# The even layer's output projection as seven half-size products with early operand sums

## The chip, the cores and the metric

The kernel runs on one core of a Trainium2 chip. The metric is device time in microseconds for one launch. A core has a matrix engine (TensorE, PE in the profile), VectorE (DVE), ScalarE (ACT), GpSimd (POOL), SyncE (SP), which issues the DMAs here, and 16 DMA engines. Matmuls read on-chip memory (SBUF) and add into PSUM banks of 128 x 512 floats.

## The reference

A decoder trunk of two layers on x of 1024 rows (s) and 1024 columns (d), in float32:

```
even: h = x @ e_w_in; A = Griffin RG-LRU of h; B = stick-breaking attention of 8 heads
      y = concat(A * silu(gate), B * silu(gate))                  # 1024 x 2048
      x1 = LayerNorm(alpha * x + y @ e_w_out)                     # e_w_out: 2048 x 1024
odd:  sliding-window attention of 16 heads with sinks, gate, output projection,
      out = LayerNorm(alpha * x1 + ...)
```

The change concerns `y @ e_w_out` with the sum and the LayerNorm (LN) around it.

## The kernel before

Every float32 product is made of three matmuls: each operand is split into a high part h (a cast) and a low part l (operand minus h), and h·h, h·l and l·h are added in one PSUM bank (`mm3`, L109). A split costs one cast and one subtraction, for weights on GpSimd (`load_piece`, L102 and L103).

The stages follow each other: loads, the recurrence half A with its projections (to about 315 us), eight attention heads (n = 0 to 7), the even output projection, the odd layer's projections with the sliding-window stage, and the odd output projection. An attention head is cut into 12 units. For a unit, TensorE makes z (L289 to 291), ScalarE two exponentials B and C, GpSimd sets one column of C (MEMSET, L299), VectorE makes the running sum C (L305) and the product B (L307), TensorE transposes B (tr, L315), and pv multiplies it by the values (L332 to 338). Between these TensorE works on filler: in heads 0 to 6 the input projections of the next head, in head 7 `early_out`.

y is kept in DRAM, split: `split_y_half` (L255) casts on ScalarE (L258), subtracts on VectorE (L259) and stores both parts. Tiles of y are named yhla and yhlb when they are made, yla and ylb when they are loaded again. The output projection (`out_proj`, L535; banks named ope) runs over 16 pieces of the contraction of 2048. For each of the two column halves (dm) and each block of 128 rows (s, eight of them) a bank is filled by 16 pieces of three matmuls 128 x 512. `early_out` (L482) does ten pieces for three row blocks of the first column half while head 7 is still running. When attention has ended, the LN constants (gb, L645), the rest of y (L267) and x (xpre, L658) are loaded, and weights (wr_e, L93) follow piece by piece. After each block of rows VectorE adds the bank to alpha * x (L544), LN runs over VectorE, ScalarE and GpSimd (`ln_a`, `ln_b`, `ln_c`), and TensorE transposes the result for the odd layer (x1tr, L673), which begins with the projections pj_ok, pj_ov and pj_oq.

Engines run their own instructions in order. Their order comes from the order of the program, from a scheduler at compile time, and from pools of tiles that make a writer wait for the last reader: 24 slots of 128 x 2 x 512, three raw tiles for weights, and PSUM banks (three pj, two z, two tr, one pv). All large DMAs are issued by SP into one queue, in order; a DMA waits for the one eight places ahead of it.

Of the kernel before, what the change touches and what calls it, by code (L numbers as in the profile page):

```python
# [18 lines left out]
P = 128  # L19
# [33 lines left out]
def trunk(ctx, tc, x, xT_in, w_even, w_even_v, w_even_out, w_gate, lru_vec,  # L53
# [381 lines left out]
    def lru_main(f):  # L435
# [25 lines left out]
        for hf in range(2):  # L461
# [11 lines left out]
    def yh_even(e, s):
        hl = yhl[("b", e - 8, s // 4) if e >= 8 else ("a", e, s // 4)]
        c = (s % 4) * P
        return hl[:, 0, c:c + P], hl[:, 1, c:c + P]

    EARLY = [13, 0, 1, 2, 3, 4, 5, 6, 7, 14]
    LATE = [8, 9, 10, 11, 12, 15]
    op0 = {}  # L480

    def early_out():  # L482
        for s in range(3):
            op0[s] = bank("pj", f"ope0_{s}")
        for idx, e in enumerate(EARLY):
            wh, wl = load_piece(w_even_out[0, e], f"f0_{e}")
            for s in range(3):
                yh_, yl_ = yh_even(e, s)
# [42 lines left out]
    ACC = ["pj", "pj", "pj", "z", "z", "tr", "tr", "pv"]  # L531
# [3 lines left out]
    def out_proj(w_src, es, yh, n_tail, tail_piece, lnp, gb, after, name, final, early=None):  # L535
# [55 lines left out]

        for dm in range(2):
# [3 lines left out]
            if dm == 0 and early:  # L596
                ps = dict(early[0])
                for ei, group in enumerate(early[1:]):
                    for idx, e in enumerate(group):
                        wh, wl = load_piece(w_src[dm, e], f"{name}{dm}_{e}")  # L600
                        for s in range(NS):
                            if ei == 0 and s in early[0]:
                                continue
                            if s not in ps:
                                ps[s] = bank(ACC[s], f"op{name}{dm}_{s}")
                            yh_, yl_ = yh(e, s)
# [352 lines left out]
```

## Time and profile before

| | us |
|---|---|
| median of three runs (lowest to highest) | 1277.57 (1277.12 to 1277.88) |
| profiled execution | 1275.71 |
| its span, first to last instruction | 1273.7 |
| TensorE busy | 1246.3, 6272 matmuls |
| VectorE, ScalarE, GpSimd busy | 770.1, 577.9, 542.4 |

Busy times are sums over all stages. Since TensorE is busy in 98% of the span, the stages in which it is not, and those in which its granted clock is lower, are to be looked for in the tables by stretches and in the waits. The mean granted clock is 0.996 of the full one.

### The profile page before, as it was taken

How to read it: one execution, taken by the hardware profiler on the slowest of the kernel's cores; microseconds unless marked ns; L12 is line 12 of the kernel's file. 1: busy time of each engine (PE TensorE's matmuls, PEld its weight loads, DVE VectorE, ACT ScalarE, POOL GpSimd, SP SyncE). 2: the span in 40 equal slices, each digit the busy share in tenths (PEclk: the TensorE clock that was granted, in tenths of full speed). 3: DMA queues.
4: the chain of work that ended last, by engine and by line, in shares of the span. 5: the costliest groups of instructions: out<-in, count | busy, mean ns of one | idle time of the engine just before them, and what ended most of it. 6: DMA issues, size and time to landing. Idle time of an engine off the chain costs nothing.

```text
span 1273.7 us, 18009 instructions
## 1 busy us (share of the span) xinstructions
PE 1246.3 (98%) x6272; PEld 1052.6 (83%) x6272; DVE 770.1 (60%) x1661; ACT 577.9 (45%) x1212; POOL 542.4 (43%) x692
## 2 busy tenths in 40 slices
PE   8999999999999999999999979999999999999997
PEld 7888788888888888888888868888788888887886
DVE  7355746645565756766658502036477777878467
ACT  5254555656343433434434300014277777778300
POOL 3333544445323323232234653536455555555440
PEclk9999999999999999999999989999999999999999
DMA  7322332234212222123128571201111111111022
GB/s 253 129 68 84 135 112 87 87 110 147 83 50 84 67 66 92 53 80 98 27 67 336 176 260 52 70 24 34 44 43 32 33 35 34 33 29 64 17 84 99
DMA packets 63306, 110.79 MB, mean 87 GB/s; under 512 B 7280, under 2 KB 25072, under 8 KB 62960
## 3 DMA queue, kind: packets, MB, share of 16 engines
q1 hardware_dynamic: 63216, 109.65, 26.5%
q8 instruction: 50, 0.82, 0.3%
q14 instruction: 40, 0.33, 0.1%
HBM read 83.40 MB, written 26.21 MB: 86 GB/s over the span
## 4 chain that ended last, share of the span: by engine, by line
PE 83%; DVE 6%; ACT 5%; DMA 2%; issue 2%; POOL 1%; SPq 0%; POOLq 0%; ACTq 0%; DVEq 0%
PE ope L110 4%; PE ope L112 4%; PE ope L111 4%; PE tr L315 2%; PE pj_g L110 2%; PE pj_g L111 2%; PE pj_g L112 2%; PE pjv L110 2%; PE pjv L111 2%; PE pjv L112 2%; PE opo L111 2%; PE opo L110 2%; PE opo L112 2%; PE pj_k L112 2%; PE pj_k L111 2%; PE pj_q L110 2%
## 5 line engine op out<-in xcount | busy, mean ns | idle before, releaser
L803 POOL TENSOR_SCALAR S<-S,sm 128x256 f32<-128x256 f32 (+1 forms) x128 | 59.9, 482 | 77.8 <-DVE sm L801 31.9
L553 ACT ACTIVATE rs<-mv,eps_t 128x1 f32<-128x1 f32 x16 | 4.7, 295 | 193.4 <-DVE mv L552 193.4
L296 ACT ACTIVATE C<-z 128x512 f32<-128x512 f32 (+3 forms) x96 | 47.3, 493 | 92.5 <-DVE z L293 77.5
L798 ACT ACTIVATE S<-S,sm 128x256 f32<-128x256 f32 (+1 forms) x128 | 62.6, 490 | 57.5 <-DVE sm L794 53.7
L544 DVE SCALAR_TENSOR_TENSOR xpre<-xpre,ope 128x512 f32<-128x512 f32 x16 | 10.8, 681 | 119.2 <-PE ope L112 119.2
L307 DVE TENSOR_TENSOR B<-B,C 128x512 f32<-128x512 f32 (+3 forms) x96 | 58.4, 608 | 10.5
L344 POOL TENSOR_TENSOR yb<-pvt,yb 128x128 f32<-128x128 f32 x32 | 15.4, 480 | 108.6 <-DVE pvt L343 85.4
L305 DVE TENSOR_TENSOR_SCAN C<-C,one 128x512 f32<-128x512 f32 (+1 forms) x64 | 54.0, 843 | 11.8 <-ACT C L296 11.6
L118 ACT CAST wt<-tr 128x512 fp32r<-128x512 f32 (+3 forms) x96 | 46.7, 486 | 29.5 <-PE tr L315 28.7
L119 DVE TENSOR_TENSOR wt<-tr,wt 128x512 fp32r<-128x512 f32 (+3 forms) x96 | 52.6, 549 | 8.0 <-ACT wt L118 7.6
L110 PE MATMUL pjv<-wv,xh 128*128 128x512 f32 x128 | 49.6, 399 | 6.2 <-ACT wv L219 6.2
L110 PE MATMUL pj_g<-xh,wh_g 128*128 128x512 f32 x128 | 51.9, 406 | 0.4 <-DVE kl L119 0.4
L110 PE MATMUL pj_k<-xh,wh_k 128*128 128x512 f32 x128 | 52.2, 408 | 0.0
L791 DVE CUSTOM_DVE_ANT_0 S<-s,bias 128x256 f32<-128x256 f32 (+1 forms) x128 | 47.4, 403 | 7.7 <-PE s L786 6.9
L110 PE MATMUL pj_og<-x1h,wh_og 128*128 128x512 f32 x128 | 51.9, 406 | 0.0
L110 PE MATMUL pj_q<-xh,wh_q 128*128 128x512 f32 x128 | 51.9, 405 | 0.0
L110 PE MATMUL pj_oq<-x1h,wh_oq 128*128 128x512 f32 x128 | 51.8, 405 | 0.0
L112 PE MATMUL pj_k<-xh,wl_k 128*128 128x512 f32 x128 | 51.6, 403 | 0.0
L111 PE MATMUL pj_og<-x1l,wh_og 128*128 128x512 f32 x128 | 51.0, 398 | 0.0
L111 PE MATMUL pjv<-wv,xh 128*128 128x512 f32 x128 | 50.5, 394 | 0.5 <-DVE wv L220 0.5
L112 PE MATMUL pj_og<-x1h,wl_og 128*128 128x512 f32 x128 | 50.8, 397 | 0.0
L111 PE MATMUL pj_k<-xl,wh_k 128*128 128x512 f32 x128 | 50.6, 395 | 0.0
(317 smaller groups left out, 4334.6 us busy)
## 6 DMA issues: line engine op xcount, KB each, us to landing
vst<-vhl SPq DMA_DIRECT2D x16, 512.0 KB, 3.7
ysta<-yhla SPq DMA_DIRECT2D x16, 512.0 KB, 3.5
yla<-ysta SPq DMA_DIRECT2D x16, 512.0 KB, 10.0
wr_e<-in_w_even_out_dram SPq DMA_DIRECT2D x32, 256.0 KB, 2.7
ystb<-yhlb SPq DMA_DIRECT2D x10, 512.0 KB, 2.9
ylb<-ystb SPq DMA_DIRECT2D x10, 512.0 KB, 6.6
xraw<-in_xT_dram SPq DMA_DIRECT2D x16, 256.0 KB, 5.4
wvraw<-in_w_even_v_dram SPq DMA_DIRECT2D x16, 256.0 KB, 4.3
```

The source lines that it names most:

```text
L110: nc.tensor.matmul(ps, wh, xh, start=start, stop=False)
L111: nc.tensor.matmul(ps, wh, xl, start=False, stop=False)
L112: nc.tensor.matmul(ps, wl, xh, start=False, stop=stop)
L118: nc.scalar.copy(h, ps)
L119: nc.vector.tensor_tensor(out=l, in0=ps, in1=h.bitcast(F32), op=ALU.subtract)
L296: nc.scalar.activation(C[:, :W], z[:, :W], AF.Sigmoid, scale=-SC)
L305: nc.vector.tensor_tensor_scan(cr, cr, one.broadcast_to([P, W]), init, ALU.mult, ALU.mult)
L307: nc.vector.tensor_tensor(out=B[:, :W], in0=B[:, :W], in1=C[:, 1:W + 1], op=ALU.mult)
L315: nc.tensor.transpose(tr[:, t * P:(t + 1) * P], B[:, t * P:(t + 1) * P], ident)
L791: nc.vector.tensor_tensor_reduce(out=Sb[:, j, lo:], in0=ps[:, j, lo:], in1=bias[:, j, lo:], scale=1.0, scalar=-BIG, op0=ALU.add, op1=ALU.m ...
L798: nc.scalar.activation(Sb[:, j, lo:], Sb[:, j, lo:], AF.Exp, bias=nm[:, j:j + 1], accum_out=den[:, j:j + 1])
L803: nc.gpsimd.tensor_scalar(out=Sb[:, j, lo:], in0=Sb[:, j, lo:], scalar1=rec[:, j:j + 1], scalar2=0.0, op0=ALU.mult, op1=ALU.add)
```

## The change

The product of y (1024 x 2048) and the weights (2048 x 1024) is cut in two in each of its three dimensions and made by the Strassen-Winograd scheme: seven products of half size in each dimension instead of eight, on sums and differences of the quarters. A11 and A21 are the two row halves of the recurrence half of y, A12 and A22 those of the attention half; b11, b21, b12 and b22 are quarters of the weights. The sums are

```
S1 = A21 + A22   S2 = S1 - A11 (as A22 - S3)   S3 = A11 - A21   S4 = A12 - S2
T1 = b12 - b11   T2 = b22 - T1 (as T3 + b11)   T3 = b22 - b12   T4 = b21 - T2
```

with the signs that the code gives them. They are made as soon as their parts are there: S3 in the recurrence stage on VectorE, T1 to T4 in each head on GpSimd (`w_sums`: four loads, four operations, four stores), S1, S2 and S4 at the end of each head on GpSimd (`y_sums`). All are kept in DRAM unsplit (`stash`, 256 KB each). `split_y_half` is gone.

The projection is 7 products of 8 steps; a step is 4 blocks of 3 matmuls 128 x 512. `prep(k)` loads the two operands of step k, casts both on ScalarE, and subtracts the y operand on VectorE (opwh) and the weight operand on GpSimd (opwl); it is called nine steps ahead. The products accumulate in two sets of banks: X (three pj and pv; named opeX) and Z (two z and two tr; opeZ), and `evac` adds banks to xpre on the way. `early_out` now does three of the four blocks of the first product. In the last product block by block is finished, with LN and transposes between. The odd layer starts with the second half of the rows. x is loaded in 16 pieces of 256 KB instead of 8 of 512 KB.

```diff
-    def split_y_half(key, hf, raw, keep):
-        hl = slot(f"yhl{key[0]}{key[1]}{hf}", F32R) if key[0] == "b" else \
-            yt(("vh", "vl")[hf], [P, 2, HALF], f"yhla{key[1]}{hf}")
-        nc.scalar.copy(hl[:, 0, :], raw)
-        nc.vector.tensor_tensor(out=hl[:, 1, :], in0=raw, in1=hl[:, 0, :].bitcast(F32), op=ALU.subtract)
...
+    def stash(kind, t, tile_):
+        yst[kind, t] = tc.dram_tile([P, HALF], F32, name=f"st{kind}{t}")
+        nc.sync.dma_start(yst[kind, t], tile_)
+
+    def w_sums(t):
...
+        for tile_, dm, e in ((b22, 1, 8 + t), (b12, 1, t), (b11, 0, t), (b21, 0, 8 + t)):
+            nc.sync.dma_start(tile_, w_even_out[dm, e])
+        sub = partial(nc.gpsimd.tensor_tensor, op=ALU.subtract)
+        sub(out=b22, in0=b22, in1=b12)
+        stash("T3", t, b22)
+        sub(out=b12, in0=b12, in1=b11)
+        stash("T1", t, b12)
+        nc.gpsimd.tensor_tensor(out=b11, in0=b22, in1=b11, op=ALU.add)
+        stash("T2", t, b11)
+        sub(out=b21, in0=b21, in1=b11)
+        stash("T4", t, b21)
...
+    def y_sums(n, hf):
+        y = ytile["b", n][:, hf, :]
+        a21, s3 = ya_in[n][:, 0, :], ya_in[n][:, 1, :]
+        if hf == 1:
+            stash("A22", n, y)
+            nc.gpsimd.tensor_tensor(out=a21, in0=a21, in1=y, op=ALU.add)
+            stash("S1", n, a21)
+            nc.gpsimd.tensor_tensor(out=s3, in0=y, in1=s3, op=ALU.subtract)
+            stash("S2", n, s3)
         else:
+            stash("A12", n, y)
+            s4 = slot(f"s4_{n}", F32)[:, 0, :]
+            nc.gpsimd.tensor_tensor(out=s4, in0=y, in1=s3, op=ALU.subtract)
+            stash("S4", n, s4)
...
+                if (i, g) == (NS - 2, 1):
+                    w_sums(n)
...
-                        for hf in range(2):
-                            for f in range(8):
-                                load_y(("a", f), hf, slot(f"yla{f}{hf}", F32R))
+                        for t in range(8):
+                            prep(t)
                         fill.add(early_out())
-                        rate[0] = 20.4 / 12
+                        rate[0] = 16.4 / 12
...
+    XB, ZB = ["pj", "pj", "pj", "pv"], ["z", "z", "tr", "tr"]
+    PRODUCTS = [("A11", (0, 0), 0), ("S3", "T3", 1), ("S2", "T2", 0), ("A22", "T4", 1), ("S1", "T1", 0),
+                ("A12", (0, 8), 1), ("S4", (1, 8), 0)]
...
+    def prep(k):
...
+            raw = wpool.tile([P, HALF], F32, tag=tag, name=f"raw{tag}{k}", bufs=5)
+            nc.sync.dma_start(raw, src)
+            hl = slot(f"op{tag}{k}", F32R)
+            nc.scalar.copy(hl[:, 0, :], raw)
+            eng = nc.vector if tag == "wh" else nc.gpsimd
+            eng.tensor_tensor(out=hl[:, 1, :], in0=raw, in1=hl[:, 0, :].bitcast(F32), op=ALU.subtract)
...
     def early_out():
...
+        for p in range(3):
+            op[0, p] = bank(XB[p], f"opeX{p}")
+        for t in range(8):
+            for p in range(3):
+                step_mm(t, p)
                 yield C_512
...
+        op[0, 3] = bank(XB[3], "opeX3")
+        for t in range(8):
+            step_mm(t, 3)
+        for k in range(8, 8 + AHEAD):
+            prep(k)
...
+            for p in range(4):
+                for t in range(8):
+                    step_mm(8 * i + t, p)
+                evac(i, p)
+                norm(p)
+                if p in (1, 2):
+                    x1_transposes(p + 1)
```

The next rows are TensorE's at the end of the last head, before: the last attention product (pv_0) with what stands ahead of it and behind it; ope are banks of the projection.

```order
L112 MATMUL ope_5_6979<-wh_e_2_7035,yla_6428 128x512
L110 MATMUL ope_3_6971<-wh_e_3_7056,yla_6414 128x512
L332 MATMUL pv_0_6907<-wt_1_0_6900,vh_5879 128x256
L333 MATMUL pv_0_6907<-wt_1_0_6900,vh_5879 128x256
L334 MATMUL pv_0_6907<-wt_1_0_6900,vl_5880 128x256
L336 MATMUL pv_0_6907<-wt_1_0_6900,vh_5879 128x256
L338 MATMUL pv_0_6907<-wt_1_0_6900,vl_5880 128x128
L110 MATMUL ope_6_6983<-wh_e_13_6967,yhlb_5821 128x512
L111 MATMUL ope_6_6983<-wl_e_13_6968,yhlb_5821 128x512
```

After, the same place; opeX is here the bank of the fourth block.

```order
L362 MATMUL pv_1_7043<-wt_3_0_7022,vl_6018 128x128
L339 MATMUL tr_0_0_7066<-ident,B_0_0_7030 128x128
L356 MATMUL pv_0_7070<-wt_1_0_7063,vh_6017 128x256
L357 MATMUL pv_0_7070<-wt_1_0_7063,vh_6017 128x256
L358 MATMUL pv_0_7070<-wt_1_0_7063,vl_6018 128x256
L360 MATMUL pv_0_7070<-wt_1_0_7063,vh_6017 128x256
L362 MATMUL pv_0_7070<-wt_1_0_7063,vl_6018 128x128
L532 MATMUL opeX_7121<-opwl_6582,opwh_6577 128x512
L533 MATMUL opeX_7121<-opwl_6582,opwh_6577 128x512
```

Projection matmuls stood between the attention products; now the products stand alone, and the projection goes on with the fourth block.

The next rows are SP's queue of DMAs behind the last head, before: ylb is y loaded again, gb the LN constants, xpre x, wr_e weights.

```order
L267 DMA ylb_6934<-ystb_3692 128x1024
L267 DMA ylb_6942<-ystb_4758 128x1024
L645 DMA gb<-in_e_ln_dram 128x2048
L267 DMA ylb_6945<-ystb_5461 128x1024
L658 DMA xpre<-in_x_dram 128x1024
L267 DMA ylb_6947<-ystb_5291 128x1024
L658 DMA xpre<-in_x_dram 128x1024 x7
L93 DMA wr_e_7_7138<-in_w_even_out_dram 128x512
L93 DMA wr_e_14_7159<-in_w_even_out_dram 128x512
```

After, the same place; stA and stS are stashes of y and its sums, rawwh and rawwl the operands of a step, here of step 13 and of step 14.

```order
L254 DMA stA_7081<-yb_6421 128x512
L687 DMA gb<-in_e_ln_dram 128x2048
L692 DMA xpre<-in_x_dram 128x512
L254 DMA stS_7085<-s_7_7083 128x512
L692 DMA xpre<-in_x_dram 128x512 x15
L517 DMA rawwh_7196<-stS_2071 128x512
L517 DMA rawwl_7201<-stT_5582 128x512
L517 DMA rawwh_7206<-stS_2336 128x512
```

The reload of y is gone, and behind x stand the operands of step 13 where the first weights behind the early pieces stood.

The last place is GpSimd's queue at the start of head 6, after (s_5 is S4 of head 5, wq6 the quarters of the weights, C the columns of the units, yb the end of a block of y).

```order
L291 TENSOR_TENSOR s_5_6129<-yb_5305,yain_5456 128x512
L323 MEMSET C_5_1_6243 128x1
L323 MEMSET C_4_1_6343 128x1
L263 TENSOR_TENSOR wq6b<-wq6b,wq6a 128x512
L265 TENSOR_TENSOR wq6a<-wq6a 128x512
L267 TENSOR_TENSOR wq6a<-wq6b,wq6a 128x512
L269 TENSOR_TENSOR wq6b<-wq6b,wq6a 128x512
L368 TENSOR_TENSOR yb_5863<-pvt_3_6332,yb_5863 128x128
L323 MEMSET C_3_0_6430 128x1
```

Four operations of `w_sums`, which are new, stand between the memsets of C of neighbouring units, and S4 ahead of them.

## Rows read from the trace of the kernel before

**Rows 1.** The page: TensorE's busy time, its granted clock by slices, the chain.
```profile
PE 1246.3 (98%) x6272; PEld 1052.6 (83%) x6272; DVE 770.1 (60%) x1661; ACT 577.9 (45%) x1212; POOL 542.4 (43%) x692
...
PEclk9999999999999999999999989999999999999999
...
PE 83%; DVE 6%; ACT 5%; DMA 2%; issue 2%; POOL 1%; SPq 0%; POOLq 0%; ACTq 0%; DVEq 0%
```

**Rows 2.** Table by stretches: span, then busy (count) of each engine, clock, DMA share, GB/s.
```profile
700.00:710.00 10.00, 9.96 (x57) 8.24 (x55) 8.32 (x14) 4.89 (x12) 7.13 (x11) 1.00 0.26 76
710.00:720.00 10.00, 9.97 (x56) 8.25 (x57) 7.81 (x15) 3.13 (x10) 8.82 (x10) 1.00 0.37 89
720.00:730.00 10.00, 10.00 (x48) 8.33 (x47) 1.18 (x3) 2.17 (x3) 2.14 (x4) 1.00 0.86 308
730.00:740.00 10.00, 10.00 (x46) 8.29 (x45) 0.00 (x0) 0.00 (x0) 5.59 (x6) 1.00 1.02 415
740.00:750.00 10.00, 3.40 (x16) 2.51 (x15) 0.00 (x0) 0.00 (x0) 0.77 (x2) 0.92 0.88 347
750.00:760.00 10.00, 10.00 (x34) 7.99 (x35) 0.00 (x0) 0.00 (x0) 9.78 (x11) 0.74 0.37 105
770.00:790.00 20.00, 20.00 (x90) 16.57 (x89) 2.69 (x5) 0.00 (x0) 7.68 (x8) 1.00 0.16 44
```

**Rows 3.** Chain of waits around the projection's start: start us, us, what.
```profile
727.71 11.23 DMA ylb<-ystb
...
739.00 9.99 DMA wr_e<-in_w_even_out_dram
```

**Rows 4.** Timeline of the DMA queue's engine: start us, us, what.
```profile
726.05 0.53 SPq L645 DMA_DIRECT2D gb<-in_e_ln_dram  x1
```

**Rows 5.** Waits from 700 to 900 us: total, times, longest, in us.
```profile
PE ope L110 <- POOL wh_e L102: 6.6, 1, 6.6
...
PE pj_ov L110 <- POOL whl_ov L102: 1.9, 1, 1.9
```

**Rows 6.** TensorE's timeline, first and last of 90 matmuls in a row.
```profile
841.74 0.39 PE L110 MATMUL ope<-whl_e,ylb 128*128 128x512 f32 x1
...
861.91 0.39 PE L110 MATMUL ope<-wh_e,yhlb 128*128 128x512 f32 x1
```

**Rows 7.** TensorE's timeline in the last attention head.
```profile
700.21 0.39 PE L289 MATMUL z<-kh,qh 128*128 128x512 f32 x1
...
724.06 0.22 PE L338 MATMUL pv<-wt,vl 128*128 128x128 f32 x1
```

**Rows 8.** Groups by shape: busy us, mean ns, idle before and its releaser.
```profile
L103 POOL TENSOR_TENSOR wl_e<-wr_e,wh_e 128x512 fp32r<-128x512 f32 x29 | 37.4, 1295 | 1.4
...
L584 POOL TENSOR_TENSOR xpre<-xpre,gb 128x1024 f32<-128x1024 f32 x8 | 19.3, 2409 | 23.0 <-ACT xpre L583 22.9
...
L103 POOL TENSOR_TENSOR wl_f<-wr_f,wh_f 128x512 fp32r<-128x512 f32 x10 | 15.2, 1520 | 0.7
...
L259 DVE TENSOR_TENSOR yhlb<-yb,yhlb 128x512 fp32r<-128x512 f32 x16 | 12.7, 791 | 12.8 <-ACT yhlb L258 12.8
...
L258 ACT CAST yhlb<-yb 128x512 fp32r<-128x512 f32 x16 | 9.9, 620 | 16.6 <-POOL C L299 13.7 <-POOL yb L344 2.9
```

**Rows 9.** Timeline of all engines, two operations side by side.
```profile
705.71 2.07 POOL L103 TENSOR_TENSOR wl_f<-wr_f,wh_f 128x512 fp32r<-128x512 f32 x1
...
706.82 1.50 DVE L307 TENSOR_TENSOR B<-B,C 128x512 f32<-128x512 f32 x1
```

**Rows 10.** Table by stretches: a middle head and the last head.
```profile
412.00:463.00 51.00, 51.00 (x277) 43.78 (x276) 33.86 (x66) 20.80 (x48) 15.60 (x24) 1.00 0.24 73
670.00:722.00 52.00, 51.78 (x297) 44.04 (x296) 41.68 (x77) 21.81 (x55) 29.67 (x37) 1.00 0.69 247
```

**Rows 11.** Timeline in a middle head: one B and its transposes.
```profile
419.66 0.56 DVE L307 TENSOR_TENSOR B<-B,C 128x384 f32<-128x384 f32 x1
...
424.93 0.49 PE L315 MATMUL tr<-ident,B 128*128 128x128 f32 x3
```

More of the change, by code (lines that the diff above doesn't have):

```diff
@@ L469, in lru_main @@
             nc.vector.tensor_tensor(out=gg, in0=xc, in1=gg, op=ALU.mult)
-            split_y_half(("a", f), hf, gg, False)
+            stash(("A11", "A21")[hf], f, gg)
+        s3 = yt("vh", [P, 2, HALF], f"s3_{f}", F32)[:, 0, :]
+        nc.vector.tensor_tensor(out=s3, in0=st["gg", 0], in1=st["gg", 1], op=ALU.subtract)
+        stash("S3", f, s3)
         yield
[L473 to L476, printed above, removed]
@@ new lines, in step_mm @@
+    def step_mm(k, p):
+        i, t = divmod(k, 8)
+        y, w = ops[k]
+        c = slice(p * P, (p + 1) * P)
+        fresh = t == 0 and i in (0, 1, 5)
+        f = partial(nc.tensor.matmul, skip_group_check=True)
+        b = op[PRODUCTS[i][2], p]
+        f(b, y[:, 0, c], w[:, 0, :], start=fresh, stop=False)
+        f(b, y[:, 0, c], w[:, 1, :], start=False, stop=False)
+        f(b, y[:, 1, c], w[:, 0, :], start=False, stop=t == 7)
+    def early_out():
+        for p in range(3):
[3 more added lines that the diff above has]
+                step_mm(t, p)
@@ L590, in ln_c @@
                 after(s, None)
+        if not final:
+            even_products(stats, ln_a, ln_b, ln_c)
+            return
         for dm in range(2):
@@ L595, in out_proj @@
             body = es[:len(es) - nt]
[L596 to L606, printed above, removed]
-                            mm3(ps[s], yh_, yl_, wh, wl, ei == 0 and idx == 0, e == early[-1][-1])
-                body = []
             for idx, e in enumerate(body):
@@ new lines, in trunk, with even_products, evac, norm @@
+    AHEAD = 9
+    def even_products(stats, ln_a, ln_b, ln_c):
+        pend = []
+        def evac(i, p):
+            half, dm, first, done = EVAC[i]
+            s = half * 4 + p
+            b = op[PRODUCTS[i][2], p]
+            xt = xpre[:, s, dm * HALF:(dm + 1) * HALF]
+            if first:
+                nc.vector.scalar_tensor_tensor(out=xt, in0=xt, scalar=ALPHA, in1=b, op0=ALU.mult, op1=ALU.add)
+            else:
+                nc.vector.tensor_tensor(out=xt, in0=b, in1=xt, op=ALU.add)
+            if done:
+                nc.vector.bn_stats(stats[s][:, dm, :], xt)
+        def norm(s):
+            mr = ln_a(s)
+            if pend:
+                ln_c(pend.pop())
+            ln_b(s, *mr)
+            pend.append(s)
+        n = 8 * len(PRODUCTS)
+        op[0, 3] = bank(XB[3], "opeX3")
[3 more added lines that the diff above has]
+            prep(k)
+        for p in range(4):
+            evac(0, p)
+        last = len(PRODUCTS) - 1
+        for i in range(1, last + 1):
+            if i in (1, 5):
+                for p in range(4):
+                    op[1, p] = bank(ZB[p], f"opeZ{i}_{p}")
+            if i < last:
+                for t in range(8):
+                    prep(8 * i + t + AHEAD)
+                    for p in range(4):
+                        step_mm(8 * i + t, p)
+                for p in range(4):
+                    evac(i, p)
+                if i == 4:
+                    for s in range(4, 8):
+                        norm(s)
+                    ln_c(pend.pop())
+                continue
+            for p in range(4):
+                for t in range(8):
+                    step_mm(8 * i + t, p)
+                evac(i, p)
+                norm(p)
+                if p in (1, 2):
+                    x1_transposes(p + 1)
+            ln_c(pend.pop())
```

90 lines of the change are left out of this document (38 added, 52 removed).

## The prediction

> **What bounds the kernel now.** I read the page first. TensorE is busy 1246.3 of 1273.7 us, it carries 83% of the chain that ended last, and its granted clock is full in all slices but one [rows 1]. So what counts is, first, how many matmuls are issued, second, where TensorE waits, third, where its clock falls. The table by stretches shows the one slice: around the start of the even output projection the engine works 3.40 of 10 us, and in the next 10 us it issues 34 matmuls where an undisturbed stretch has 46 [rows 2]. The chain of waits gives the reason: a load of y (ylb) and then one of weights (wr_e) end last, 11.23 and 9.99 us [rows 3]. They stand in one queue behind each other, with the LN constants (1 MB) and x (4 MB); DMA moves 415 GB/s in that stretch, so the queue is full, not slow [rows 2, 4]. The list of waits puts 6.6 us of TensorE's idleness there, and 1.9 us at the start of the odd layer behind a weight cast on GpSimd [rows 5].
>
> **Fewer matmuls.** Before: 16 pieces of the contraction x 16 output tiles x 3 = 768. After: 7 products x 8 steps x 4 blocks x 3 = 672, all 128x512. In the projection 90 matmuls in a row start from 841.74 to 861.91 us [rows 6]: 20.17 / 89 = 0.2266 us each. 96 fewer give **-21.8 us**. Nothing lies beside them; TensorE is the bound there.
>
> **The stall at the projection's start.** The y reload (5 MB) goes away, and the weights of steps 8 to 12 are loaded ahead of the LN constants and x instead of behind them. That removes the 6.6 us of waiting and the slow clock behind it, (46 - 34) x 0.2266 = 2.7 us: **-9.3 us**. What is late next is step 13. Its loads now stand where wr_e stood: behind the last stash of y, 1 MB of constants, 4 MB of x and one more stash, with its own 0.5 MB about 6 MB. At 415 GB/s [rows 2] that is 14.5 us; before, the constants are issued 2.0 us behind the last attention product (726.05 against 724.06) [rows 4, 7]. With attention over at 716.5 (below) they land at 733, and with cast, subtraction and landing step 13 is ready about 736.5 to 737.5. TensorE comes to it after 24 + 5 x 12 = 84 matmuls from 717.4, at 736.4. Bounds 0 and 3 us; I take **+0.5**.
>
> **The last head.** Before, TensorE has ready work to the end of attention: by the order of instructions 127 projection matmuls stand ahead of the end of the last product at 724.2 [rows 7]. After, early_out has only 72 (three banks, eight steps), and the fourth block needs the bank of the attention product itself. So 55 x 0.2266 = 12.5 us of work are gone from this stretch: if TensorE alone set its pace, attention would end at 711.7. VectorE sets it. Behind the z product at 700.21 [rows 7] stand 64 of the 127; after, all 72 stand ahead of it, and twelve short products (some 1.4 us) move behind, so that this z comes at 700.21 + 9 x 0.2266 - 1.4 = 700.8. VectorE has 8.32 + 7.81 + 1.18 = 17.3 us to do from 700 on [rows 2], about 1.5 of it behind the last product. Back to back that ends the products at 716.5. TensorE idles 716.5 - 711.7 = 4.8 us in pieces, and 0.9 more until the bank is read out. Bounds: 0.9 (TensorE's pace) and 13.4 (attention no earlier than before). I take **+5.7**, next to VectorE's rows.
> Pieces of idleness can cost the clock too: 6.6 us in one piece were followed by 2.7 us of loss [rows 2, 5]. Bounds 0 and 2.7, since these pieces are shorter; **+1.3**.
>
> **Operands streamed.** Each step (12 matmuls, 2.72 us) wants two loads (0.5 MB, 1.2 us at 415 GB/s), two casts on ScalarE at 0.62, a subtraction on VectorE at 0.79 and one on GpSimd at 1.30 to 1.52 [rows 8]. Each stays under 2.72, on engines that are nearly empty there (VectorE 2.69 us in 20) [rows 2]. With nine steps prepared ahead I count **0**; without the cover the price is what one step exceeds 2.72 by, and nothing in the rows does.
> At this place VectorE and GpSimd subtract side by side, and the trace shows them slowing each other: a GpSimd subtraction of 2.07 us overlaps a VectorE multiplication of 512 columns that takes 1.50 us [rows 9], where one of 384 columns alone takes 0.56 [rows 11]. The Trainium skill's page "SBUF — State Buffer" (Who interferes with whom) says that the two share a pair of ports, so that a VectorE instruction with two SBUF inputs contends with a GpSimd one that reads SBUF. The trace agrees: by it the two subtractions of a step may run one behind the other, 0.79 + 1.52 = 2.3 us, still under 2.72, and the sum would stay. In the heads the same rule speaks against the change, below.
>
> **Attention heads.** GpSimd gets seven more 128x512 operations a head: w_sums four, y_sums three, 7 x 1.30 to 1.52 = 9.1 to 10.6 us. VectorE and ScalarE each lose two (y splits, 0.79 and 0.62) [rows 8]. A middle head has GpSimd 15.60 of 51 us busy, so 25 to 26 after. The last head of before has GpSimd at 29.67 and VectorE at 41.68 of 52 us, more than the new heads will have, and TensorE was idle 0.22 us in it [rows 10]. Results also come some microseconds before they are used: one B ends at 419.66 + 0.56 = 420.2, its transposes start at 424.93 [rows 11]. So **0**; the upper bound is rival A. The extra DMA of a head, 2.3 MB of stores and 1.5 MB of loads, is 3.8 MB in 51 us, 75 GB/s beside 73 [rows 10], far from 415.
>
> **The recurrence stage.** ScalarE's casts and VectorE's subtractions of y go (16 each), 8 subtractions for S3 come: **0**, below nothing by a microsecond at most.
>
> **Start of the odd layer.** The last product finishes rows block by block, with LN under it. After the last block TensorE has 24 projection matmuls and 16 transposes, about 7 us, until the next transposes need the last LN. By the rows that LN is two VectorE passes of 0.79, ScalarE over 1024 columns 1.24, GpSimd's multiplication 2.41 and VectorE's addition 1.58 [rows 8], 6.8 us, with the small operations between them some 8 to 9 (estimate); a cast and a subtraction on GpSimd then stand ahead of whl_ov. That is a gap of 2 to 3 us where 1.9 and some short ones were [rows 5]; the sliding-window stage then starts with 38 filler matmuls ahead of its first transposes instead of 60. Bounds -2.5 and +4; **+1.5**.
>
> **Sum**: -21.8 - 9.3 + 5.7 + 0.5 + 1.3 + 1.5 = -22.1 us. The profiled execution took 1275.71 us (span 1273.7 and 2.0 around it), so 1253.6; the median of the runs is 1.9 us above it: **1255.5**. With all bounds at their best -32.7 (1244.9), at their worst -8.0 (1269.6).
>
> **Rivals.**
> A, the other side: *GpSimd blocks the heads.* The four w_sums stand in one block ahead of the small memsets of C and of yb, in order and behind a wait for their loads. At 1.30 each they are 5.2 us, stretched to 2.07 each [rows 9] they are 8.3; the slack is about 4.7 us [rows 11]. For it: GpSimd's stretched operation, and that the next units' C waits behind. Against: a last head with more work on both engines that did not wait [rows 10]. At 4 us in each of 8 heads it costs 32: 1287.5. From 2.8 us a head on the change loses. The Trainium skill's rule above would lengthen this block and VectorE's work with it.
> B, *the ramp eats the gain*: attention ends hardly earlier (+12), the clock stays low through the fourth block (+2.7), step 13 is late by 3: -21.8 - 9.3 + 12 + 2.7 + 3 + 1.5 = -11.9, 1265.7. For it: the last head is without filler for some 16 us. Against: VectorE's rows leave no work for 724.
> C, *the ramp costs nothing*: TensorE's pace ends attention (+0.9), no clock loss, no wait at step 13, the odd start as before: -30.2, 1247.4. For it: the stretched VectorE operations there [rows 9] shrink, as GpSimd no longer casts weights. Against: 17.3 us of VectorE work.
> D, *it doesn't stream*: operands come at more than 2.72 us a step, say 2.95, and the product saving is gone over the 47 remaining steps (11 us): 1266. No row shows an engine over 2.3.
>
> **How the numbers follow.** Forecast 0.62, A 0.08, B 0.16, C 0.10, D 0.04. About what a measurement of this kernel can tell from no change is 0.2%, 2.6 us. All but A end clearly faster; of A some cases end near zero. So faster 0.90, same 0.03, slower 0.07. The range reaches over the forecast's own spread (1250 to 1261) to C and B: 1246 to 1267; A is left out.
>
> **What would show it.** Right: 96 fewer TensorE instructions; no wait for wr_e or raw13 over 3 us around 735; idle pieces of 4 to 7 us in all between 700 and 718; the fourth block's first matmul (opeX3) near 717.4; the first odd matmul (pj_ok) near 858 (717.4 + 600 x 0.2266 + 32 transposes and the small losses); heads still 51 to 52 us with GpSimd near 26. Wrong: TensorE waits for B or C in the heads; spaced matmuls in the products behind opwl; a granted clock below full in more than one slice; a gap over 5 us at the odd start.

## The result and the profile after

| | before | after |
|---|---|---|
| median of the runs (lowest to highest), us | 1277.34 (1276.54 to 1277.88) | 1261.39 (1261.12 to 1262.78) |
| span of the profiled execution, us | 1273.7 | 1259.4 |
| matmul instructions | 6272 | 6176 |

The ratio of after to before is 0.9878, with an interval of 0.9861 to 0.9895: 16 us faster, 1.2%. The forecast was 1255.5, 22 us faster; the time lies in the range, 6 us above the forecast. On the page, the busy times, the clock by slices and the chain:

```profile
PE 1228.9 (98%) x6176; PEld 1038.1 (82%) x6176; DVE 855.7 (68%) x1705; ACT 623.5 (50%) x1291; POOL 631.1 (50%) x720
...
PEclk9999999999999999999999999999999999999999
...
PE 85%; DVE 6%; DMA 2%; ACT 2%; issue 2%; POOL 2%; POOLq 0%; SPq 0%; DVEq 0%; ACTq 0%
```

96 matmul instructions are gone, and with them 17.4 us of TensorE's busy time (before in [rows 1]). TensorE leads the chain as before. The table by stretches shows where it still waits (span, busy and count of PE, PEld, DVE, ACT, POOL, clock, DMA share, GB/s):

```profile
412.00:463.00 51.00, 51.00 (x277) 43.72 (x276) 35.25 (x64) 20.44 (x48) 26.05 (x33) 1.00 0.40 130
670.00:700.00 30.00, 26.99 (x145) 22.96 (x144) 27.01 (x42) 16.09 (x37) 15.22 (x18) 0.94 0.60 196
700.00:710.00 10.00, 9.89 (x62) 8.60 (x61) 9.74 (x15) 4.44 (x11) 7.41 (x6) 1.00 0.63 217
710.00:720.00 10.00, 6.87 (x46) 5.50 (x44) 9.49 (x19) 5.17 (x15) 1.13 (x6) 1.00 0.12 45
720.00:730.00 10.00, 7.18 (x31) 5.52 (x30) 6.71 (x17) 6.30 (x16) 7.29 (x7) 0.83 0.37 121
730.00:740.00 10.00, 10.00 (x45) 8.25 (x44) 5.54 (x6) 0.60 (x2) 6.43 (x5) 1.00 1.02 365
740.00:750.00 10.00, 9.64 (x41) 7.34 (x41) 2.57 (x3) 3.80 (x7) 2.64 (x2) 1.00 1.05 387
870.00:880.00 10.00, 8.04 (x46) 6.41 (x44) 6.76 (x11) 5.34 (x10) 9.19 (x6) 1.00 0.17 54
```

In a stretch that spans a middle head TensorE makes as many matmuls as before (277), without a gap, although GpSimd went from 15.60 to 26.05 us [rows 10]. The hole at 740 to 750 [rows 2] has shrunk from 6.6 us to 0.4. A new hole is at 670 to 730: 9.1 us of idleness in the rows from 670 to 730, and the granted clock twice below full. In the rows from 670 to 720 VectorE is busy 46.2 of 50 us, where before it was 41.7 of 52 [rows 10]. TensorE's timeline has the last attention product, the first matmul of the fourth block, and the first projection of the odd layer:

```profile
724.83 0.22 PE L362 MATMUL pv<-wt,vl 128*128 128x128 f32 x1
726.08 0.47 PE L532 MATMUL opeX<-opwl,opwh 128*128 128x512 f32 x1 [1.03 <-DVE pvt L367]
...
868.38 0.48 PE L110 MATMUL pj_ok<-x1h,whl_ok 128*128 128x512 f32 x1
```

Attention ends at 725.0, where it ended at 724.2 before [rows 7] and where the prediction had 716.5. From there to the odd layer it takes 143.4 us. The start of the odd layer waits little (TensorE's waits from 860 to 900 us: total, times, longest):

```profile
PE x1tr L708 <- DVE xpre L641: 1.2, 1, 1.2
...
PE pj_ov L110 <- POOL whl_ov L102: 0.8, 1, 0.8
```

Before, 1.9 us stood at the second of these places [rows 5].

### The profile page after: what moved, and what is told of

Same layout as the page of the kernel before. It is cut to its first block, busy times and chain, and to the rows that moved or that the text cites. A ratio compares the mean times of both kernels' runs of the same rounds, so it can differ in the third digit from the quotient of the medians.

```text
span 1259.4 us, 18456 instructions
## 1 busy us (share of the span) xinstructions
PE 1228.9 (98%) x6176; PEld 1038.1 (82%) x6176; DVE 855.7 (68%) x1705; ACT 623.5 (50%) x1291; POOL 631.1 (50%) x720
## 4 chain that ended last, share of the span: by engine, by line
PE 85%; DVE 6%; DMA 2%; ACT 2%; issue 2%; POOL 2%; POOLq 0%; SPq 0%; DVEq 0%; ACTq 0%
PE pjv L110 2%; PE pjv L111 2%; PE pjv L112 2%; PE pj_k L112 2%; PE pj_k L111 2%; PE pj_q L110 2%; PE pj_k L110 2%; PE pj_oq L110 2%; PE pj_q L112 2%; PE pj_oq L111 2%; PE pj_q L111 2%; PE pj_oq L112 2%; PE pj_og L110 2%; PE pj_g L110 2%; PE pj_og L111 2%; PE pj_g L112 2%
## 5 line engine op out<-in xcount | busy, mean ns | idle before, releaser
L521 POOL TENSOR_TENSOR opwl<-rawwl,opwl 128x512 fp32r<-128x512 f32 x56 | 88.8, 1611 | 36.1 <-ACT opwl L519 35.9
L521 DVE TENSOR_TENSOR opwh<-rawwh,opwh 128x512 fp32r<-128x512 f32 x56 | 72.4, 1326 | 20.2 <-ACT opwh L519 20.1
L331 DVE TENSOR_TENSOR B<-B,C 128x512 f32<-128x512 f32 (+3 forms) x96 | 72.2, 752 | 10.1 <-DVE C L329 0.5
L329 DVE TENSOR_TENSOR_SCAN C<-C,one 128x512 f32<-128x512 f32 (+1 forms) x64 | 60.7, 949 | 16.7 <-ACT C L320 16.6
L110 PE MATMUL pjv<-wv,xh 128*128 128x512 f32 x128 | 49.9, 401 | 7.7 <-ACT wv L219 7.7
L329 DVE TENSOR_TENSOR_SCAN C<-C,C,one 128x512 f32<-128x512 f32 x32 | 42.0, 1313 | 18.3 <-ACT C L320 18.2
L519 ACT CAST opwh<-rawwh 128x512 fp32r<-128x512 f32 x56 | 34.8, 621 | 36.9 <-DMA rawwh<-stS 15.5
L532 PE MATMUL opeX<-opwl,opwh 128*128 128x512 f32 x128 | 51.0, 402 | 1.0 <-DVE pvt L367 1.0
L534 PE MATMUL opeX<-opwl,opwh 128*128 128x512 f32 x128 | 51.5, 403 | 0.0
L533 PE MATMUL opeX<-opwl,opwh 128*128 128x512 f32 x128 | 51.5, 403 | 0.0
L339 PE MATMUL tr<-ident,B 128*128 128x128 f32 x288 | 47.3, 273 | 4.2 <-DVE B L331 4.1
```

Of the source, the lines that this page charges most:

```text
L110: nc.tensor.matmul(ps, wh, xh, start=start, stop=False)
L329: nc.vector.tensor_tensor_scan(cr, cr, one.broadcast_to([P, W]), init, ALU.mult, ALU.mult)
L331: nc.vector.tensor_tensor(out=B[:, :W], in0=B[:, :W], in1=C[:, 1:W + 1], op=ALU.mult)
L521: eng.tensor_tensor(out=hl[:, 1, :], in0=raw, in1=hl[:, 0, :].bitcast(F32), op=ALU.subtract)
L532: f(b, y[:, 0, c], w[:, 0, :], start=fresh, stop=False)
L533: f(b, y[:, 0, c], w[:, 1, :], start=False, stop=False)
```

## The experiments

Each run edits the kernel after the change. The two columns on the right frame the last head in the profiled execution: the start of the last matmul of its query projection (pj_q), and the start of the last matmul of an attention product (pv, which ends 0.2 us later). Between the two lies also the gate projection of the last head (48 matmuls), which ends head 6. In e8, e10 and e11 it is moved into the last head, and the query projection ends later for that, so that there the first of the two columns can't be set beside the other rows. The runs of before that were made beside each group of experiments have medians of 1277.34 to 1278.36 us, so between groups a difference of ratios says more than one of times.

| kernel | median us | ratio to before (interval) | last pj_q | last pv |
|---|---|---|---|---|
| before | 1277.34 | 1 | 656.8 | 724.1 |
| after | 1261.39 | 0.9878 (0.9861, 0.9895) | 658.9 | 724.8 |
| e1_presplit | 1257.77 | 0.9844 (0.9829, 0.9859) | 658.3 | 719.9 |
| e2_subs_gpsimd | 1262.44 | 0.9875 (0.9858, 0.9891) | 659.2 | 725.4 |
| e3_double | 1267.15 | 0.9914 (0.9900, 0.9929) | 658.1 | 730.1 |
| e4_w7_early | 1260.35 | 0.9860 (0.9845, 0.9875) | 658.8 | 722.9 |
| e6_nosplits | 1255.65 | 0.9837 (0.9817, 0.9857) | 660.2 | 718.5 |
| e7_wv | 1261.41 | 0.9869 (0.9856, 0.9883) | 658.9 | 724.8 |
| e8_g7 | 1259.30 | 0.9851 (0.9838, 0.9865) | 662.6 | 721.6 |
| e9_heads | 1263.73 | 0.9886 (0.9873, 0.9900) | 658.6 | 725.6 |
| e10_g7_nosplits | 1250.22 | 0.9788 (0.9775, 0.9802) | 665.8 | 713.5 |
| e11_all | 1250.08 | 0.9782 (0.9768, 0.9795) | 666.5 | 714.4 |
| e12_loads | 1252.60 | 0.9805 (0.9791, 0.9818) | 660.9 | 719.2 |

### What bounds the last head

After's timeline of all engines at the start of the last head (start us, us, engine, line, what, idle before and its releaser):

```profile
667.43 4.08 DVE L521 TENSOR_TENSOR opwh<-rawwh,opwh 128x512 fp32r<-128x512 f32 x3
...
667.64 5.02 POOL L521 TENSOR_TENSOR opwl<-rawwl,opwl 128x512 fp32r<-128x512 f32 x3 [3.15 <-ACT opwl L519]
...
671.63 2.11 DVE L329 TENSOR_TENSOR_SCAN C<-C,one 128x512 f32<-128x512 f32 x1
...
677.51 1.70 DVE L521 TENSOR_TENSOR opwh<-rawwh,opwh 128x512 fp32r<-128x512 f32 x1
...
679.13 1.61 DVE L331 TENSOR_TENSOR B<-B,C 128x384 f32<-128x384 f32 x1
...
680.88 0.30 PE L339 MATMUL tr<-ident,B 128*128 128x128 f32 x1 [3.01 <-DVE B L331]
```

Three y subtractions (opwh) take 4.08 us of VectorE beside three weight subtractions of GpSimd; a fourth stands directly ahead of a product B, itself stretched to 1.61, and TensorE waits 3.01 us for that B. So the eight steps that run in this head bring eight subtractions to VectorE, in the head in which it had the least room. Theory V is that VectorE sets the end of this head and that these subtractions come on top of its work. It has two rivals: the chain of the attention is too long in itself once the filler is used up (L), or it is GpSimd that stretches VectorE's work (G).

**e1_presplit**: A11 is split in the recurrence stage.

```diff
-            stash(("A11", "A21")[hf], f, gg)
+            if hf == 0:
+                hl = yt("vl", [P, 2, HALF], f"a11s{f}")
+                nc.scalar.copy(hl[:, 0, :], gg)
+                nc.vector.tensor_tensor(out=hl[:, 1, :], in0=gg, in1=hl[:, 0, :].bitcast(F32), op=ALU.subtract)
...
+            if i == 0 and tag == "wh":
+                hl = slot(f"op{tag}{k}", F32R)
+                nc.sync.dma_start(hl.bitcast(F32), src)
```

> The changed kernel with A11 split already in the recurrence stage (one cast on ScalarE and one subtraction on VectorE per tile there, 512 KB stored and loaded), so that the eight steps that run in the last attention head need no cast and no subtraction for y. Theory V (VectorE bounds the last head, and the eight subtractions, 9.2 us there in the changed kernel, came on top of it): the last attention product ends 6 to 9 us earlier than the 725.0 of the changed kernel, about 716 to 719, the time is 1253 to 1256 us. Rival L (the last head runs out of TensorE work, and the length of its dependent chain sets its end, whatever VectorE does besides): the end stays within 2 us of 725.0, the time is 1259 to 1262. Rival G (it is GpSimd that stretches VectorE's attention work): 2 to 4 us earlier, 1257 to 1259.

Measured: 1257.77 us, the last product at 719.9 instead of 724.8, 4.9 us earlier, 4.3 of it in the last head itself (61.6 from the last pj_q instead of 65.9). L, which allowed 2 us, falls. V had 6 to 9 and G 2 to 4: the end lies between the two, and the time in G's range (1257 to 1259). What became of the rest shows in VectorE's groups from 664 to 690 us (busy us, mean ns, idle before), first of after:

```profile
L521 DVE TENSOR_TENSOR opwh<-rawwh,opwh 128x512 fp32r<-128x512 f32 x8 | 9.2, 1168 | 0.0
L329 DVE TENSOR_TENSOR_SCAN C<-C,one 128x512 f32<-128x512 f32 (+3 forms) x5 | 6.4, 1278 | 0.7 <-ACT C L320 0.7
L331 DVE TENSOR_TENSOR B<-B,C 128x512 f32<-128x512 f32 (+3 forms) x5 | 4.5, 905 | 0.2
```

and of e1_presplit:

```profile
L331 DVE TENSOR_TENSOR B<-B,C 128x512 f32<-128x512 f32 (+3 forms) x7 | 8.1, 1153 | 0.8
```

The 9.2 us of subtractions are gone, but the products B beside GpSimd's weight subtractions have become longer: those of 512 columns alone (the lines mix shapes) take 1267 ns in the mean, of four, instead of 694, of two. GpSimd takes a part of what is freed, so V and G seem to hold together. e1 takes eight casts from ScalarE as well; but VectorE waited only 0.7 us for ScalarE in this stretch (the second line), so that the casts are no likely cause.

**e2_subs_gpsimd**: the eight y subtractions on GpSimd.

```diff
-            eng = nc.vector if tag == "wh" else nc.gpsimd
+            eng = nc.vector if tag == "wh" and k >= 8 else nc.gpsimd
```

> The changed kernel with the y subtractions of steps 0 to 7 on GpSimd instead of VectorE; nothing else. Theory V: 9.2 us leave VectorE in the last head, but GpSimd gets 8 more of 1.3 to 1.6 us and stretches VectorE's attention work for as long: the attention ends 2 to 6 us earlier, 1255 to 1259 us. Rival L: no change within 2 us, 1259 to 1263. Rival G: later by 2 to 6 us, since GpSimd does more: 1263 to 1267.

Measured: 1262.44 us, the last product at 725.4. That is L's number; V had it 2 to 6 us earlier and G as much later, and both are missed. The table by stretches says why (670 to 700 us, columns as above):

```profile
670.00:700.00 30.00, 28.42 (x157) 23.63 (x156) 27.02 (x37) 16.16 (x38) 28.48 (x24) 1.00 0.67 201
```

GpSimd is now busy 28.48 of 30 us, and VectorE, relieved of eight operations, is still busy 27.02 (27.01 in after, with five operations more in the stretch). The work that left VectorE came back as stretching. With e1, where the work left both engines, this is against L, against V alone and against G alone, and for V and G together (VG).

**e3_double**: each of the eight subtractions twice.

```diff
+            if tag == "wh" and k < 8:
+                eng.tensor_tensor(out=hl[:, 1, :], in0=raw, in1=hl[:, 0, :].bitcast(F32), op=ALU.subtract)
```

> The changed kernel with each y subtraction of steps 0 to 7 done twice on VectorE. Theory V: eight more operations of 0.69 to 1.4 us on the bounding engine: attention ends 5.5 to 11 us later, 1267 to 1272 us. Rival L: under 2 us, 1260 to 1263. Rival G: about 2 us, since the added work is not GpSimd's.

Measured: 1267.15 us, 5.8 more; from the last pj_q to the last pv 72.0 us, 6.1 more than after. VectorE has hardly any gap (670 to 700 us):

```profile
670.00:700.00 30.00, 25.55 (x128) 21.18 (x127) 29.12 (x44) 13.26 (x30) 15.90 (x16) 0.94 0.62 199
```

A second set of eight subtractions costs 6.1 us at the end of the head, 0.76 each; taking the first set away gave 4.3 (e1). Between the two lies the price of the eight that the change brought.

**e4_w7_early**: the last w_sums in head 6.

```diff
-                if (i, g) == (NS - 2, 1):
+                if (i, g) == (NS - 2, 1) and n < 7:
                     w_sums(n)
+                if (n, i, g) == (6, 4, 0):
+                    w_sums(7)
```

> The changed kernel with the four GpSimd operations of w_sums for the last piece made in head 6 instead of in the last head. Theory V: the VectorE operations that they stretch in the last head (four products B of 1.10 to 1.53 us around 700 to 710 where 0.3 to 0.7 is usual, 3.2 us in all) become short: attention ends 2 to 3.5 us earlier, 1258 to 1259.5 us. Rival L: 0 to 1 us. Rival G: 4 us or more, below 1257.5.

Measured: the last product at 722.9, 1.9 us earlier, just under V's range; 1260.35 us, above V's 1259.5, in runs that overlap with those of after. G's 4 us fall. So this step is shown by the trace, not by the time. VectorE's products B from 690 to 722 us, in after and in e4_w7_early:

```profile
L331 DVE TENSOR_TENSOR B<-B,C 128x512 f32<-128x512 f32 (+3 forms) x12 | 9.9, 825 | 0.6
```

```profile
L331 DVE TENSOR_TENSOR B<-B,C 128x512 f32<-128x512 f32 (+3 forms) x12 | 6.5, 553 | 0.4
```

3.4 us of stretching are gone from the same twelve products, of which 1.9 reach the end.

**e6_nosplits**: e1 and e4, and b11 split in w_sums too (the kernel also splits and stores b11 in each head).

```diff
+        hl = slot(f"b11s{t}", F32R)
+        nc.scalar.copy(hl[:, 0, :], b11)
+        sub(out=hl[:, 1, :], in0=b11, in1=hl[:, 0, :].bitcast(F32))
+        yst["B11", t] = tc.dram_tile([P, 2, HALF], F32, name=f"stB11{t}")
+        nc.sync.dma_start(yst["B11", t], hl.bitcast(F32))
```

> The changed kernel with both operands of steps 0 to 7 split earlier (A11 in the recurrence stage, b11 with a cast on ScalarE and a subtraction on GpSimd in each head's w_sums) and the last w_sums made in head 6. So no split and no w_sums is left in the last head. Theory VG (VectorE bounds the last head: its own work, the eight subtractions, and the stretching by GpSimd, which the first runs showed to fill up what a freed VectorE gains): VectorE has only its own 42 us there, the last attention product ends at 714 to 717.5, the time is 1250 to 1254 us. Rival L (the chain's length alone bounds it): no earlier than 719, 1256 to 1258.

Measured: 1255.65 us (runs from 1254.44 to 1261.75), 1.65 above VG's range and just under L's, and from the last pj_q to the last pv 58.3 us, 7.6 less than after. The end in absolute time, 718.5, lies in neither range, a microsecond behind VG's; the last pj_q is 1.3 us later than in after, and counted from there the end is in VG's. Its stretches:

```profile
670.00:700.00 30.00, 30.00 (x176) 26.11 (x175) 25.14 (x50) 13.81 (x34) 6.54 (x12) 1.00 1.00 385
700.00:710.00 10.00, 9.85 (x61) 8.44 (x59) 5.90 (x11) 4.28 (x10) 0.60 (x3) 1.00 0.01 5
710.00:720.00 10.00, 6.00 (x40) 4.93 (x40) 7.43 (x21) 4.33 (x14) 3.85 (x6) 1.00 0.21 79
```

Up to 700 TensorE is never idle; then VectorE has room (5.90 of 10), and at 710 to 720 TensorE works 6 of 10 us and VectorE 7.43: no projection matmuls stand between the attention's any more, and this stretch fits L.

**e8_g7**: the last head's gate projection moved from head 6 into the last head.

```diff
+    def last_fill():
+        get = w_ftile(w_even, 16 + 7, "g7")
+        yield from proj_half(get, 1, "g7", evac_gate(("b", 7)))
+        for t in range(4):
+            prep(t)
+        yield from proj_half(get, 0, "g7", evac_gate(("b", 7)))
+        for t in range(4, 8):
+            prep(t)
+        yield from early_out()
```

> The changed kernel with the 48 gate matmuls of the last head (g7) moved from the end of head 6 into the last head, ahead of the early output projection. Theory VG with the reading that TensorE lacks work there: head 6 becomes 10.9 us shorter, since TensorE bounds it, the last head takes the time that VectorE needs, now with TensorE busy in it; idle and slow clock of some 9 to 11 us go: 1251 to 1254 us. Rival H (VectorE or GpSimd bounds head 6 as well, as soon as it is shorter): head 6 gets at most 4 us shorter, 1257 to 1261.

Measured: 1259.30 us, 2 less, in rival H's range. VectorE does not let the head become much shorter:

```profile
670.00:700.00 30.00, 29.08 (x160) 24.54 (x159) 28.67 (x38) 18.20 (x39) 17.48 (x17) 1.00 0.62 202
700.00:710.00 10.00, 6.33 (x28) 4.65 (x27) 9.49 (x14) 2.67 (x7) 6.43 (x8) 0.92 0.59 181
```

It is busy 28.67 of 30 and 9.49 of 10 us. More work for TensorE is worth little here as long as VectorE bounds.

**e10_g7_nosplits**: e6 and e8 together.

> The kernel without splits in the last head (e6) with the gate matmuls of the last head moved into it as well (e8). Without the splits VectorE has room in the last head (5.90 of 10 us at 700 to 710) and TensorE is what lacks work at 710 to 720 (6.0 of 10). Theory VG, second half (once VectorE is relieved, the missing TensorE work is what is left): the 4 us of idleness are filled, attention ends 3 to 5 us earlier than at 718.5, 1251 to 1253.5 us. Rival H (VectorE bounds head 6 as soon as that is shorter, as the run with g7 alone showed at 640 to 700): 0 to 1.5 us, 1254 to 1256.

Measured: 1250.22 us, better than expected, 5.4 under e6, where the same step brought 2.1 on the kernel after. By the ratios that is 6.3 against 3.4 us, and the difference of the two gains is within their intervals; in the profiled executions the last product comes 5.0 against 3.2 us earlier.

```profile
670.00:700.00 30.00, 28.30 (x163) 23.94 (x162) 28.38 (x54) 16.14 (x40) 11.25 (x19) 1.00 0.78 277
700.00:710.00 10.00, 10.00 (x62) 8.84 (x61) 5.06 (x13) 2.56 (x8) 3.01 (x3) 1.00 1.03 408
710.00:720.00 10.00, 10.00 (x53) 8.50 (x53) 5.84 (x10) 5.92 (x13) 5.69 (x5) 1.00 0.71 254
```

From 700 on TensorE is busy throughout at the full clock. Attention ends at 713.7 us. Both halves of VG count: VectorE relieved, and work for TensorE.

### The queue behind the last head

In e6_nosplits one wait stood behind the ramp (TensorE's waits, 715 to 760 us):

```profile
PE opeZ L551 <- ACT opwl L538: 1.7, 1, 1.7
```

**e11_all** and **e12_loads** load x in groups, and the constants later:

```diff
-    nc.sync.dma_start(gb, e_ln.rearrange("(o a) d -> o a d", o=1).broadcast_to([P, 2, D]))
...
+        load_xpre(0, 0)
         for k in range(8, 8 + AHEAD):
             prep(k)
+        load_xpre(1, 1)
...
+            if i == 3:
+                nc.sync.dma_start(gb, e_ln.rearrange("(o a) d -> o a d", o=1).broadcast_to([P, 2, D]))
```

> e6 with the loads as in e11, without the moved gate. If the queue is the cause: 2 to 3 us less than e6, 1252.5 to 1254 us; rival: within 1 us of 1255.65.

> e10 with the LN constants and x loaded in groups of 1 MB, each one product ahead of its use, so that the operands of step 13 and behind stand ahead of most of them. If the queue behind 4 MB of x and 1 MB of constants is what leaves TensorE idle around 730 to 750 (1.9 us there in e6, and a lower clock), it goes: 2 to 3.5 us less than e10, 1248 to 1251 us. Rival: step 13 is late because its raw tiles come free late, not because of the queue: within 1 us of e10.

Measured: 1252.60 us on e6 (3.1 less in the medians, in the range of the first theory; 1.7 less in the profiled executions, in which TensorE's 1.9 us of idleness from 730 to 750 have gone), and 1250.08 on e10 (0.1 less, the rival's number). In e10 the waits around 740 are gone already; why, was not tested. So loading in groups gained something in e6 and nothing in e10.

### The heads

**e9_heads**: four more GpSimd subtractions ahead of w_sums in heads 0 to 6, into a tile that nobody reads.

```diff
+        if t < 7:
+            dmy = slot(f"dmy{t}", F32)
+            for i in range(4):
+                sub(out=dmy[:, i % 2, :], in0=b22, in1=b12)
```

> The changed kernel with four more 128x512 subtractions on GpSimd in each of heads 0 to 6 (their results are not used), just ahead of w_sums. If GpSimd has room in the heads (26 of 52 us busy), nothing: 1260 to 1263 us. Rival A (the block of GpSimd operations delays C, and the slack of some 3 to 5 us is used up by the four that the change put there): 5 to 6 us more per block, 1 to 4 us a head, 1268 to 1290.

Measured: the middle head is as long as it was, with GpSimd at 35.23 us:

```profile
412.00:463.00 51.00, 51.00 (x277) 43.75 (x276) 38.94 (x63) 20.32 (x48) 35.23 (x39) 1.00 0.42 135
```

The last query projection starts at 658.6 (658.9 after). So rival A of the prediction falls with a margin of four more operations. The median is 2.3 us higher all the same, 0.7 above what was expected (1.0 us by the ratios, whose intervals overlap); in the profile that arises behind the heads (last pv 0.8 later, and 2.0 us of waits for operands at 740 to 750). Why, the runs don't tell.

### The recurrence stage

The first key projection of the profiled execution starts 2.7 us later than before (293.5 against 290.8). The table by stretches shows where, by TensorE's count of matmuls, of 0.2266 us each. Before:

```profile
0.00:20.00 20.00, 15.31 (x61) 12.58 (x62) 13.76 (x22) 14.30 (x22) 1.29 (x12) 1.00 0.89 319
120.00:140.00 20.00, 18.01 (x76) 13.73 (x75) 16.03 (x20) 11.40 (x19) 8.94 (x8) 1.00 0.59 197
```

and after:

```profile
0.00:20.00 20.00, 15.03 (x56) 12.25 (x57) 14.13 (x22) 14.32 (x22) 1.51 (x12) 1.00 0.93 326
120.00:140.00 20.00, 17.27 (x69) 13.77 (x68) 14.44 (x18) 11.35 (x17) 8.57 (x7) 0.91 0.53 184
```

Five matmuls (1.1 us) are missing after 20 us already, in a stretch where both kernels are the same: runs with one code in this stage start the first key projection at 292.7 to 293.8, so this part is the execution's. Seven (1.6 us) are missing from 120 to 140, at one wait. Before, timeline of all engines:

```profile
124.49 1.28 DVE L466 TENSOR_TENSOR_SCAN xc<-ri,xc,t 128x512 f32<-128x512 f32 x1
...
125.83 0.33 SPq L215 DMA_DIRECT2D wvraw<-in_w_even_v_dram  x1
...
128.88 1.28 POOL L456 TENSOR_TENSOR ri<-ri,xc 128x512 f32<-128x512 f32 x1 [6.12 <-ACT ri L446]
...
129.36 0.50 PE L110 MATMUL pjv<-wv,xh 128*128 128x512 f32 x1 [1.52 <-ACT wv L219]
```

After, the same place:

```profile
125.03 0.69 DVE L495 TENSOR_TENSOR gg<-xc,gg 128x512 f32<-128x512 f32 x1
...
125.16 1.71 POOL L482 TENSOR_TENSOR ri<-ri,xc 128x512 f32<-128x512 f32 x1 [1.25 <-ACT ri L472]
...
125.64 2.31 DVE L492 TENSOR_TENSOR_SCAN xc<-ri,xc,t 128x512 f32<-128x512 f32 x1
...
128.01 0.33 SPq L215 DMA_DIRECT2D wvraw<-in_w_even_v_dram  x1
...
131.94 0.50 PE L110 MATMUL pjv<-wv,xh 128*128 128x512 f32 x1 [2.73 <-ACT wv L219]
```

A load of value weights (SPq) follows the second scan, whose buffer it takes, and TensorE waits for it. Before, ScalarE's casts of y stood ahead of ri, so that GpSimd's operation on ri came at 128.88, behind the scan. Now it comes at 125.16, beside the scan; the scan takes 2.31 us instead of 1.28, the load goes out later, and one wait of 2.73 us stands where three of 1.52, 0.19 and 0.28 stood. The granted clock from 130 to 140 us is then 0.83 instead of 1.00. Another reading is that the stores of the sums in the queue hold up the loads.

**e7_wv**: the stores of the second tile behind the loads.

```diff
             for d in range(ND):
                 load_wv(1, d)
+            for a in late:
+                stash(*a)
```

> The changed kernel with the three stashes of the second recurrence tile issued behind the loads of the value weights (wvraw) instead of among them. Theory Q (these stores stand in the queue between the loads and make one wait of 2.7 us out of two short ones, after which the granted clock is lower): the clock is full from 120 to 140 us, the first pj_k starts 1.5 to 2.7 us earlier than at 293.5, the time is 1258.5 to 1260 us. Rival: the loads come as late anyway, since their buffers come free late: first pj_k at 293 to 294, 1261 to 1262.

Measured: 1261.41 us, the first pj_k at 293.5, nothing gained; the scan is still 2.31 us and the wait 2.87. That reading falls. In e1_presplit, where a cast of y is back, the scan takes 1.28 us and the wait is 1.99. The scan's stretching was not taken away alone, and it explains only a part. e6_nosplits and e10_g7_nosplits have the same code in this stage, with the cast, and in both the scan takes 1.28 us. In e6_nosplits:

```profile
120.00:140.00 20.00, 18.04 (x73) 14.43 (x72) 13.37 (x18) 11.29 (x18) 8.27 (x9) 0.91 0.58 197
```

and in e10_g7_nosplits:

```profile
120.00:140.00 20.00, 17.75 (x78) 14.05 (x77) 14.17 (x18) 12.19 (x18) 8.88 (x9) 1.00 0.57 197
```

Four of the seven matmuls (0.9 us) are back in e6, and all of them in e10, where the clock is full though the wait is 2.24 us in one piece. The other runs with this code have 71 and 72 (e1, e11 and e12). So the scan's stretching explains 0.9 us at most; what the clock does there, and the rest, stay open.

## Why the prediction was right and where it was not

- **Fewer matmuls** (-21.8): right; 96 fewer, and no engine kept TensorE from it: from 750 to 830 it issues 45 or 46 matmuls in 10 us, at the full clock. TensorE's busy time fell by 17.4 us only; in e10, where the clock is full from 670 to 760, it fell by 22.2 (to 1224.1), so the difference fits matmuls at a lower clock.
- **The stall at the start** (-9.3, and +0.5 for step 13): right. 0.4 us of waiting is left at 740 to 750. That it is so little is in part chance: in e4, e6, e8 and e9 TensorE waits 1.5 to 2.0 us for an operand around 730 to 750, still within the bounds. (The 6 MB of the prediction are 6.29 in the profile's units, 15.2 us at 415 GB/s and not 14.5.)
- **The last head** (+5.7, clock +1.3): this step failed in its size. I took VectorE's work from the rows of before, 17.3 us from 700 on, and ended attention at 716.5, 59.7 us behind the last pj_q; it took 66.1. The eight y subtractions of the first product were counted only under the streamed operands, at 0.79 us against 2.72 of matmuls, although these eight steps run in the last head, where VectorE sets the end. They cost 4.3 (e1) to 6.1 us (e3) there, the w_sums of this head 1.9 (e4), and without splits and w_sums it takes 58.5 us (e6), 1.2 less than the prediction had. With the wait ahead of the fourth block the step measures 12.2 us: 725.0 - 711.7 - 2.1 (the later start) + 1.0. That is 6.5 us over the 5.7 that I took, most of the distance from the forecast; the step's own upper bound, 13.4, held. Rival B's first part, attention ending hardly earlier, came true, and what I held against it, that VectorE has no work for so long, was the mistake.
- **Operands streamed** (0): right from step 8 on. From 750 to 790 VectorE and GpSimd are both busy the whole time, since they are catching up: in the trace they make 24 and 25 subtractions in these 40 us, a step in some 1.6 us, where TensorE needs one in 2.72. The groups are longer than I took them:

```profile
L521 POOL TENSOR_TENSOR opwl<-rawwl,opwl 128x512 fp32r<-128x512 f32 x56 | 88.8, 1611 | 36.1 <-ACT opwl L519 35.9
L521 DVE TENSOR_TENSOR opwh<-rawwh,opwh 128x512 fp32r<-128x512 f32 x56 | 72.4, 1326 | 20.2 <-ACT opwh L519 20.1
```

  1.33 and 1.61 us (0.79 and 1.30 to 1.52 in [rows 8]); the two overlap, and a step of both stays under 2.72. The Trainium skill's page "SBUF — State Buffer" (Who interferes with whom) has the two engines share ports; the trace agrees, and here the rule was worth more than I gave it: not in the stream, but in the last head and in the recurrence stage.
- **Attention heads** (0): right, 26.05 us of GpSimd with no wait, and e9 shows room beyond that.
- **The recurrence stage** (0): wrong by some 1.6 us in this execution. Taking ScalarE's casts away moved a GpSimd operation beside a scan; that explains 0.9 of it at most; the rest, the clock of 0.83 among it, stays open.
- **Start of the odd layer** (+1.5): too dear. From the first pj_ok to the end it takes 391.0 us, before 391.2; the wait for whl_ov went from 1.9 to 0.8 us, with 1.2 ahead of it.

The span of the profiled execution is 7.8 us above the forecast's (1251.6): 2.1 ahead of the last head, 6.5 in it, -1.7 in the odd layer, and the 0.9 that are left behind the last head, where the clock was 0.83 at the fourth block. The median lies only 5.9 above the forecast, in the main since the profiled execution of before lay 1.9 us under its median, and that of after 0.3.

## What to carry to other kernels

When a change lets work run early, beside another stage, count each of its instructions on the engine that bounds that stage, not on the one that the change is about; here eight subtractions, each of under a microsecond when alone, took back a fifth to a quarter of the forecast gain. Work that two engines do at each other's cost was not made cheaper by moving it from one to the other (e2); it had to go to another time (e1, e6). And filling the matrix engine paid more after the engine that bounds had been relieved: the same move ended attention 3.2 us earlier without that and 5.0 with it, and both together beat the change by 11 us.

## What the runs showed of the hardware

A VectorE scan of 512 columns took 1.28 us alone and 2.31 beside a GpSimd operation. That operation itself took 1.71 us instead of 1.28, but a VectorE multiplication was running when it started (125.03 to 125.72). The ends fit one engine waiting for the other: 125.72 + 1.28 = 127.00, where GpSimd ended at 126.87, and 126.87 + 1.28 = 128.15, where the scan ended at 127.95. This is read from one place, and no run was made for it.

Nearly the same idleness of TensorE at the first value product went with either clock over 130 to 140 us: 1.99 us in three pieces with the full one (before), 1.99 in one piece with 0.83 (e1), 2.73 in one piece with 0.83 (after), and 2.24 in one piece with the full one (e10). So neither the amount nor the number of pieces decides in these runs.
